# Local means of a pooling branch: shifted additions on GpSimd in place of products with banded matrices

## Chip, cores and metric

The kernel runs on one core of a Trainium2 chip. The metric is the device time of one execution in microseconds. Three runs of the kernel before took 1716.43, 1716.89 and 1719.67 us; their median is 1716.89 us.

## What is computed

The reference is a transformer of two layers over 256 latent tokens and 256 context tokens of width 1024, in float32. Each layer has a half feed-forward block, a mixing block and a second half feed-forward block. The mixing block projects the normalised tokens with `w_in` and puts three branches beside one another: neighbourhood attention (4 heads), a pooling branch (256 features), and grouped-query attention (GQA, 8 query heads, 2 key heads, with rotary positions on the latent tokens). `w_out` brings them back to 1024 features. In the last layer the context tokens only give keys and values, so pooling runs three times in all: for the latent and the context half in layer 0, and for the latent half in layer 1.

The pooling branch is what the change touches. Its 256 features fall into four groups of 64 with windows of 2, 4, 8 and 16 tokens:

```python
def _pool_mix(u, w_pool, scale):
    ...
    lo = jnp.clip(t - win // 2, 0, n)
    hi = jnp.clip(t - win // 2 + win, 0, n)
    sums = cs[:, hi, g_idx] - cs[:, lo, g_idx]
    mean = sums / (hi - lo).astype(jnp.float32)[None, :, :, None]
    y = (mean - u32.reshape(bn, n, POOL_GROUPS, POOL_GC)).astype(u.dtype)
    y = jnp.einsum('blgc,gcd->blgd', y, w_pool)
    return y.reshape(bn, n, POOL_WIDTH) * scale
```

Here `cs` is the running sum of u over the tokens. For each token the mean over a window of its neighbours is taken, u itself is subtracted, and each group is multiplied by a 64 x 64 matrix and scaled.

## The kernel before

The code names the engines PE (TensorE), ACT (ScalarE), DVE (VectorE), POOL (GpSimd) and SP (the queue that loads the weights). Activations lie with features on partitions and tokens along the row; columns 0 to 255 are the latent half (v = 0) and 256 to 511 the context half (v = 1). The large products are done three times over (`mm3`, L344 to L351): weights and activations are split into a high part and the rest, both in a reduced float32, and high x high, high x rest and rest x high are added up. Weights come from HBM into a raw buffer and are split into a slot by ACT (the high part, L306) and DVE (the rest, L309). `take` asks for the next slot in the order in which `attn_stream` (L607) queued them, and `done` gives a slot back and starts the next split.

The order of the work on each engine is the order in which the program issues it. A planner in the builder sets it: `tick` (L105) advances a clock by the estimated PE time of each product, and `later(us, fn)` issues a step when that clock has come to its due time.

In `attention` (L675), the keys, the queries of neighbourhood attention and its values `va` come first. Then `run` (L928) goes through a list of jobs. In layer 0 there are six of neighbourhood attention, then twelve of GQA; in layer 1 four and eight. For each job n the scores are issued (`scores`, L824, with the products in L838 and L839 and the softmax in `soft`), then filler work for as long as the table FILL says, and then `flip` (L867), which transposes the probabilities of job n - 2 on PE and copies them on ACT (L886). At the end of job n the queries of jobs n + 1 and n + 2 are split (`queries`, L815; L725 on ACT and L726 on DVE) if they are ready.

The filler work comes in pieces from `piece` (L1048). First comes `rest_in` (L964), the projections that are left:

- four q chunks of 128 features for GQA, each of 24 products of 512 columns (256 in layer 1) and yielded in four pieces. ACT takes each out of PSUM (L978) and squares it (L980); its statistics are taken on PE 3.0 later (L985).
- After every two chunks, `q_post(j)` is due 3.0 later. It calls `rotate` (L731): a product with a rotation matrix on PE (L736), a product with the sines on DVE (L739), a product with the cosines on POOL (L740), and, due 1.5 later, their addition on DVE (L743). Then `norm`, due 2.0 later, takes a reciprocal square root by a chain of small DVE instructions (L388 to L397, and L960). GQA jobs of a chunk wait for it by the flag `turned`.
- u, by `token_major` (L791): with tokens on partitions, one block of 128 tokens at a time, activations as the stationary operand and the weights as the moving one, 24 products of 256 columns for each block.

When `rest_in` has ended, pieces are `pv` (L901, the product of probabilities and values), `pooled` for each half, the products of modulation (L181, weights `w_ada` from HBM by SP, L157) and `rest_out` (L993), which multiplies what does not depend on GQA with `w_out`.

`pooled(v)` (L1007) multiplies u by banded matrices that hold the window weights minus the identity: for each group two products of 128 x 128 (L1015) and two of 8 columns (L1016, L1017) for the windows that reach over the boundary of the two token blocks. These are plain float32. The result is copied by ACT to y (L1020); 3.0 later `fin` multiplies it by the pooling weights (L1025), and ACT and DVE scale and split the result (L1029, L1030). The bands come by two loads for each layer (L808) into two temporary buffers, and the edges by one (L642).

POOL also clears the zero halves of the key tiles (`key_tile`, L707; the GQA keys at job 2) and other buffers, and issues some loads.

Of the kernel before, what the change touches and what calls it, by code (L numbers as in the profile page):

```python
# [9 lines left out]
F32 = mybir.dt.float32  # L10
# [26 lines left out]
T2K = 12  # L37
# [13 lines left out]
def dit_kernel(  # L51
# [2 lines left out]
    x, c, ctx_in, c_ctx, w_ada, b_ada, norm_g,  # L54
    ffn1_up, ffn1_down, ffn2_up, ffn2_down, w_in, w_out,
    na_rpb, pool_w, pool_scale, q_norm_g, k_norm_g, final_g,
    k_ident, k_rot, k_rope, k_mask, k_pool, k_edge,
    out,
):
    nc = tc.nc  # L60
# [25 lines left out]
    gsc = const.tile([128, 6, KD, 2], F32, name="gsc")  # L86
    hgt = const.tile([128, 4, KD, 2], F32, name="hgt")
    bm = const.tile([128, 2048], F32, name="bm")
    edge = const.tile([128, 2, 4, 8], F32, name="edge")
    pwbd = const.tile([128, 2, 128], F32, name="pwbd")  # L90

    def mm_bank(dt=F32):
        return ps_mm.tile([128, 512], dt, tag="mm", name="mm")
# [32 lines left out]
    def add_main(src3, shape, splits):  # L126
        stream.append(("main", src3, shape, splits))
# [228 lines left out]
    def acol(a, k, lo, hi):  # L356
        return a[:, 0, k, lo:hi], a[:, 1, k, lo:hi]
# [249 lines left out]
    def attn_stream(l, ada=()):  # L607
        ada = list(ada)
        w = w_in[l]
        c0 = lambda v: v[:, :, 0:128]  # L610
        c1 = lambda v: v[:, :, 128:256]
        k0 = lambda v: v[:, 0:4, :]
        k1 = lambda v: v[:, 4:8, :]

        def blk(lo):
            return w[:, lo:lo + 256].rearrange("(k p) f -> p k f", p=128)

        def fill():
            if ada:
                add_ada(*ada.pop(0))  # L620
        add_main(blk(256), (KD, 256), [c0, c1])
        add_main(blk(1536), (KD, 256), [c0, c1])
        add_main(blk(0), (KD, 256), [c0, c1])
        add_main(blk(512), (KD, 256), [k0, k1])
        for j in range(2):
            srcs = [w[:, 1024 + t * 256 + j * 128:1024 + t * 256 + j * 128 + 128].rearrange("(k p) f -> p k f", p=128) for t in range(2)]
            cc = [lambda v, i=i: v.rearrange("p k (t c) -> p (k t) c", t=2)[:, :, i * 64:(i + 1) * 64] for i in range(2)]
            add_main(srcs, (KD, 256), cc)
        add_main(blk(768), (KD, 256), [k0, k1])
        for part in range(2):  # L630
            for dq in range(2):
                for _ in range((0, 4, len(ada), 0)[2 * part + dq]):
                    fill()
                src = w_out[l][part * 512:(part + 1) * 512, dq * 512:(dq + 1) * 512].rearrange("(k p) d -> p k d", p=128)
                add_main(src, (4, 512), [lambda v: v[:, :, 0:256], lambda v: v[:, :, 256:512]])

    def attn_prep(l):

        if l == 0:
            ACT.dma_start(out=mask, in_=k_mask)  # L640
            ACT.dma_start(out=rot, in_=k_rot)
            ACT.dma_start(out=edge, in_=k_edge)  # L642
# [32 lines left out]
    def attention(l, a, both):  # L675
# [8 lines left out]
        def carve(n, pat, **kw):  # L684
            r = B[:, o0[0]:o0[0] + n].rearrange(pat, **kw)
            o0[0] += n
            return r
        va = carve(1024, "p (b f) -> p b f", b=4)
        u = carve(1024, "p (b f) -> p b f", b=4)
        qc = carve(2048, "p (c t) -> p c t", c=4)  # L690
        kc = carve(512, "p t -> p t")
        vc = carve(512, "p (b f) -> p b f", b=4)
        vcT = carve(512, "p t -> p t")
        A = a["t"]
        bmv = bm.rearrange("p (t h k) -> p t h k", t=2, h=4)
        O = [None]
# [105 lines left out]
        for _ in token_major(va, 4):  # L802
            pass


        pmd = [tmp.tile([128, 512], F32, tag="t2k", bufs=T2K, name="pmd") for _ in range(2)]
        for b in range(2):
            ACT.dma_start(out=pmd[b].rearrange("p (g t) -> p g t", g=4), in_=k_pool[b])  # L808


        rq8 = small.tile([128, 40], F32, tag="rq8", bufs=1, name="rq8")
# [151 lines left out]

        def rest_in():  # L964

            qst.append(mm_bank())
            for j in range(2):
                sl = [take(), take()]
# [17 lines left out]
                    later(3.0, qstat)  # L986
                    yield
                later(3.0, lambda j=j: q_post(j))
            yield from token_major(u, nb)

        gate = modT[:, l * 72 + 40:l * 72 + 48, :]

# [12 lines left out]
                done()  # L1005

        def pooled(v):  # L1007
            ps = mm_bank()
            pv_ = ps.rearrange("p (c t) -> p c t", c=2)
            for g in range(4):  # L1010
                r0 = 64 * (g % 2)
                o = pv_[r0:r0 + 64, g // 2, :]
                ug = [u[:, 2 * v + tb, g * 64:(g + 1) * 64] for tb in range(2)]
                for tb in range(2):
                    PE.matmul(out=o[:, tb * 128:(tb + 1) * 128], lhsT=ug[tb], rhs=pmd[tb][:, g * 128:(g + 1) * 128], start=(g < 2 and tb == 0), stop=False)  # L1015
# [6 lines left out]
            def fin():
                ps2 = mm_bank()
                for ch in range(2):
                    PE.matmul(out=ps2[:, ch * TX:(ch + 1) * TX], lhsT=pwbd[:, ch, :], rhs=y[:, ch * TX:(ch + 1) * TX], start=True, stop=True)  # L1025
                for ch in range(2):
                    s = colsB[:, 104 + 2 * l + ch:105 + 2 * l + ch]
                    oh, ol = acol(O[0], 2 + ch, v * TX, v * TX + TX)
                    ACT.activation(out=oh, in_=ps2[:, ch * TX:(ch + 1) * TX], func=AF.Copy, scale=s)  # L1029
                    DVE.scalar_tensor_tensor(out=ol, in0=ps2[:, ch * TX:(ch + 1) * TX], scalar=s, in1=oh.bitcast(F32), op0=ALU.mult, op1=ALU.subtract)  # L1030
                missing[0] -= 1
# [268 lines left out]
def _constants():  # L1300
# [17 lines left out]
    kcol = np.arange(64)  # L1318
    w0 = np.clip(col - 8, 0, 48)[:, None]
    mask = ((kcol[None] >= w0) & (kcol[None] < w0 + 16)).astype(np.uint32)  # L1320
    pool = np.zeros((256, 4, 256), np.float32)
    for g, w in enumerate((2, 4, 8, 16)):
        for t in range(256):
            lo, hi = max(t - w // 2, 0), min(t - w // 2 + w, 256)
            pool[lo:hi, g, t] = np.float32(1.0) / np.float32(hi - lo)
            pool[t, g, t] -= np.float32(1.0)
    blocks = np.stack([pool[0:128, :, 0:128], pool[128:256, :, 128:256]])
    edge = np.stack([pool[0:128, :, 128:136], pool[128:256, :, 120:128]], axis=1)
    return {"k_ident": ident, "k_rot": rot, "k_rope": rope, "k_mask": mask, "k_pool": np.ascontiguousarray(blocks), "k_edge": np.ascontiguousarray(edge)}
# [27 lines left out]
```

## Time and profile before

| what | value |
|---|---|
| median of three runs | 1716.89 us |
| the profiled execution's own time | 1716.95 us |
| its span in the trace | 1715.2 us |
| granted clock, mean | 0.99 |
| PE busy | 1675.8 us, 98% of the span |
| DVE busy | 1024.0 us, 60% |
| ACT busy | 663.5 us, 39% |
| POOL busy | 40.0 us, 2% |

The span is counted from the first instruction to the last; the 1.75 us between it and the execution's time lie around them. Times in rows of the profile are microseconds from the span's start unless marked ns. In a row of the timeline the first number is the start, the second the length, then come the engine, the line of the kernel, the operation, output and inputs with their size, the count, and in brackets the idle time before it with what ended it. Matmuls overlap in these rows: the time that one costs is the distance from its start to that of the next. Layer 0's mixing block runs from about 395 to 600 us, layer 1's from about 1341 to 1500 us. The program's names `q`, `u`, `va` and others are parts of one tile, and show up as `qkv`.

### The profile page before, as it was taken

To read this page: it belongs to the slowest core of one execution; us is meant where nothing else is said; L and a number is where in the kernel's file an instruction comes from. 1 tells how busy PE (TensorE), PEld (TensorE's weight loads), DVE (VectorE), ACT (ScalarE), POOL (GpSimd) and SP (SyncE) were. 2 spreads that over 40 slices of the span, in tenths; PEclk is the share of its full clock that TensorE was granted. 3 is DMA by queue.
4 is the path that set the end of the run, shared out by engine and by line. 5 is a ranking of instruction groups with operands and counts; after the bars stand their busy time and mean duration, and the time that the engine had idled before them with its cause. 6 is when DMAs were issued, how large, how long until landed. Compare 5 with 4: busy or idle time off the path is not lost.

```text
span 1715.2 us, 23680 instructions
## 1 busy us (share of the span) xinstructions
PE 1675.8 (98%) x9512; PEld 1420.5 (83%) x9512; DVE 1024.0 (60%) x1748; ACT 663.5 (39%) x1087; POOL 40.0 (2%) x60
## 2 busy tenths in 40 slices
PE   6999999999999999999999999999999999989998
PEld 4778888889886798888888898888888987779998
DVE  5667666666555676665764567545434656565554
ACT  4432223324556643223233243223222356644443
POOL 0000200000010000000000000020000000000000
PEclk8999999999999999999999999999999999989999
DMA  9755556531305325453653334555433134556561
GB/s 319 207 166 172 161 161 189 166 129 50 111 28 193 107 67 184 148 154 135 184 178 99 98 105 166 160 154 180 134 99 98 50 111 148 185 139 193 171 198 50
DMA packets 295335, 246.48 MB, mean 144 GB/s; under 512 B 9377, under 2 KB 262442, under 8 KB 293176
## 3 DMA queue, kind: packets, MB, share of 16 engines
q1 hardware_dynamic: 292680, 241.30, 45.6%
q0 software_dynamic: 1088, 2.15, 0.5%
q8 instruction: 75, 1.23, 0.3%
q10 hardware_dynamic: 1456, 1.52, 0.3%
q14 instruction: 36, 0.29, 0.1%
HBM read 243.88 MB, written 2.00 MB: 143 GB/s over the span
## 4 chain that ended last, share of the span: by engine, by line
PE 90%; DVE 4%; DMA 3%; ACT 2%; issue 1%; SPq 0%; DVEq 0%; ACTq 0%
PE mm L348 27%; PE mm L350 27%; PE mm L349 27%; PE mm L912 1%; PE aux L878 1%; DVE w L309 1%; DMA raw<-in_w_ada_dram 1%; DMA ada_raw<-in_w_ada_dram 1%; PE ada L181 1%; PE mm L838 1%; PE mm L839 1%; DVE ada_acc L221 1%; PE ada L229 1%; ACT w L306 1%; PE aux L409 0%
## 5 line engine op out<-in xcount | busy, mean ns | idle before, releaser
L348 PE MATMUL mm<-act,w 128*128 128x512 f32 (+1 forms) x2592 | 910.4, 351 | 5.7 <-ACT act L437 3.3
L350 PE MATMUL mm<-act,w 128*128 128x512 f32 (+1 forms) x2592 | 903.3, 348 | 1.9 <-DVE w L309 1.9
L349 PE MATMUL mm<-act,w 128*128 128x512 f32 (+1 forms) x2592 | 903.4, 349 | 1.1 <-DVE act L431 0.9
L348 PEld LDWEIGHTS mm<-act,w 128*128 128x128 f32 x2592 | 493.2, 190 | 86.7 <-issue 15.9
L350 PEld LDWEIGHTS mm<-act,w 128*128 128x128 f32 x2592 | 493.1, 190 | 64.4 <-DVE w L309 2.5
L349 PEld LDWEIGHTS mm<-act,w 128*128 128x128 f32 x2592 | 493.4, 190 | 63.1 <-DVE act L431 1.6
L309 DVE TENSOR_TENSOR w<-raw,w 128x1024 fp32r<-128x1024 f32 (+1 forms) x312 | 371.1, 1199 | 244.5 <-ACT w L306 243.9
L306 ACT CAST w<-raw 128x1024 fp32r<-128x1024 f32 (+1 forms) x312 | 315.0, 1023 | 120.5 <-PE mm L350 98.4
L221 DVE SCALAR_TENSOR_TENSOR ada_acc<-ada_raw,sc,ada_acc 128x512 f32<-128x512 f32 x308 | 216.1, 746 | 50.9 <-DMA ada_raw<-in_w_ada_dram 27.3
L558 ACT CAST act<-gf 128x512 fp32r<-128x512 f32 (+1 forms) x87 | 49.7, 572 | 317.5 <-DVE gf L555 317.5
L461 DVE SCALAR_TENSOR_TENSOR hT<-mm,hgt,hT 128x256 f32<-128x256 f32 x168 | 75.1, 480 | 96.9 <-PE mm L350 96.6
L552 ACT ACTIVATE sil<-mm 128x512 f32<-128x512 f32 (+1 forms) x87 | 47.7, 548 | 214.2 <-PE mm L350 204.1
L555 DVE TENSOR_TENSOR gf<-sil,mm 128x512 f32<-128x512 f32 (+1 forms) x87 | 54.4, 625 | 93.5 <-PE mm L350 77.7
L559 DVE TENSOR_TENSOR act<-gf,act 128x512 fp32r<-128x512 f32 (+1 forms) x87 | 54.9, 631 | 55.5 <-ACT act L558 55.5
L374 ACT ACTIVATE sq<-hT 128x256 f32<-128x256 f32 (+1 forms) x52 | 25.6, 492 | 108.5 <-DVE hT L461 108.5
L437 ACT ACTIVATE act<-nt,modT 128x256 fp32r<-128x256 f32 x88 | 43.4, 508 | 49.4 <-DVE nt L436 49.3
L219 ACT ACTIVATE ada_acc<-ada_raw,sc 128x512 f32<-128x512 f32 x44 | 29.6, 717 | 47.9 <-DMA ada_raw<-in_w_ada_dram 37.1
L855 DVE TENSOR_REDUCE nm<-mm 128x1 f32<-128x512 f32 (+1 forms) x60 | 41.0, 686 | 4.4 <-PE mm L839 3.7
L863 ACT ACTIVATE P<-mm,nm,rq 128x512 f32<-128x512 f32 (+1 forms) x48 | 33.7, 708 | 21.9 <-DVE nm L860 18.9
L431 DVE SCALAR_TENSOR_TENSOR act<-nt,modT,act 128x256 fp32r<-128x256 f32 x88 | 41.3, 480 | 1.3 <-ACT act L437 1.3
L436 DVE SCALAR_TENSOR_TENSOR nt<-hT,gsc,aux 128x256 f32<-128x256 f32 x88 | 40.8, 476 | 1.8 <-PE aux L416 1.2
L660 POOL DMA_DIRECT2D braw<-tab x32 | 19.5, 619 | 780.7 <-DVE gf L555 604.3
(149 smaller groups left out, 885.4 us busy)
## 6 DMA issues: line engine op xcount, KB each, us to landing
raw<-in_ffn_up_dram SPq DMA_DIRECT2D x172, 512.0 KB
ada_raw<-in_w_ada_dram SPq DMA_DIRECT2D x192, 256.0 KB
raw<-in_ffn_down_dram SPq DMA_DIRECT2D x32, 1024.0 KB
raw<-in_w_ada_dram SPq DMA_DIRECT2D x16, 1024.0 KB
raw<-in_ffn_down_dram SPq DMA_DIRECT2D x16, 768.0 KB
raw<-in_w_in_dram SPq DMA_DIRECT2D x10, 1024.0 KB
raw<-in_w_out_dram SPq DMA_DIRECT2D x8, 1024.0 KB
raw<-in_w_ada_dram SPq DMA_DIRECT2D x12, 512.0 KB
```

What stands on the lines that cost most here:

```text
L221: DVE.scalar_tensor_tensor(out=o, in0=raw, scalar=col, in1=o, op0=ALU.mult, op1=ALU.add)
L306: ACT.copy(out=wh, in_=sl)
L309: DVE.tensor_tensor(out=wl, in0=sl, in1=wh.bitcast(F32), op=ALU.subtract)
L348: PE.matmul(out=ps, lhsT=wh, rhs=ah, start=start and i == 0, stop=False)
L349: PE.matmul(out=ps, lhsT=wh, rhs=al, start=False, stop=False)
L350: PE.matmul(out=ps, lhsT=wl, rhs=ah, start=False, stop=stop and i == last)
L437: ACT.activation(out=acol(a, k, v * TX, v * TX + TX)[0], in_=t, func=AF.Identity, bias=modT[:, l * 72 + 3 * n * 8 + k, v:v + 1])
L461: DVE.scalar_tensor_tensor(out=hT[:, k, cols], in0=ps, scalar=gate[:, k, v:v + 1], in1=hT[:, k, cols], op0=ALU.mult, op1=ALU.add)
L552: ACT.activation(out=s[:, 0:n], in_=pa[:, 0:n], func=AF.Silu)
L555: DVE.tensor_tensor(out=u[:, 0:n], in0=s[:, 0:n], in1=pb[:, 0:n], op=ALU.mult)
L558: ACT.copy(out=gh, in_=uv)
L559: DVE.tensor_tensor(out=gl, in0=uv, in1=gh.bitcast(F32), op=ALU.subtract)
```

## The change

u is now projected with features on partitions, as the q chunks are, and ahead of them: two chunks of 128 features with 24 products of 512 columns each (256 in layer 1), in four pieces each. Its weights move ahead of those of q in the queue of weights. ACT copies the result into rows of 272 columns for each half, of which 8 on each side are zero.

The window sums are then shifted additions along these rows on POOL, in `window_means`, which is issued at the start of the first q piece, for each half. Sums of 2 come from u and u shifted by one; sums of 4 from two sums of 2; sums of 8 from two of 4; sums of 16 from two of 8. Each group's sum is multiplied by a table of reciprocal counts, and u is subtracted; the result takes u's place. `pooled` then has only the product with the pooling weights left, without the copy of y and without the wait of 3.0, and the planner charges 0.86 for it in place of 1.7 (its second product was not charged before). The loads of bands and edges go; a table of 256 KB is loaded for each layer. Two small memsets on POOL clear the margins of u.

```diff
@@ attn_stream
         add_main(blk(512), (KD, 256), [k0, k1])
+        add_main(blk(768), (KD, 256), [c0, c1])
         for j in range(2):
...
-        add_main(blk(768), (KD, 256), [k0, k1])
@@ attention
-        u = carve(1024, "p (b f) -> p b f", b=4)
+        u = carve(4 * UW, "p (c v t) -> p c v t", c=2, v=2)
+        sums1 = carve(2 * UW, "p (c t) -> p c t", c=2)
+        sums2 = carve(2 * UW, "p (c t) -> p c t", c=2)
...
-        pmd = [tmp.tile([128, 512], F32, tag="t2k", bufs=T2K, name="pmd") for _ in range(2)]
-        for b in range(2):
-            ACT.dma_start(out=pmd[b].rearrange("p (g t) -> p g t", g=4), in_=k_pool[b])
+        ACT.dma_start(out=count, in_=k_count)
+        for p0 in (0, UW - 8):
+            POOL.memset(u[:, :, :, p0:p0 + 8], 0.0)
+
+        def window_means(v):
+            uv, lo, hi = u[:, :, v], slice(0, 64), slice(64, 128)
+            inner = slice(8, 8 + TX)
+            def add(o, a, b):
+                POOL.tensor_tensor(out=o, in0=a, in1=b, op=ALU.add)
+            add(sums1[:, :, 1:272], uv[:, :, 0:271], uv[:, :, 1:272])
+            add(sums2[:, :, 2:271], sums1[:, :, 1:270], sums1[:, :, 3:272])
+            means = [(lo, 0, sums1), (hi, 0, sums2), (lo, 1, sums1), (hi, 1, sums2)]
+            for i, (r, ch, src) in enumerate(means):
+                if i == 2:
+                    add(sums1[:, 1, 4:269], sums2[:, 1, 2:267], sums2[:, 1, 6:271])
+                if i == 3:
+                    add(sums2[hi, 1, 8:264], sums1[hi, 1, 4:260], sums1[hi, 1, 12:268])
+                o = src[r, ch, inner]
+                POOL.tensor_tensor(out=o, in0=o, in1=count[r, ch], op=ALU.mult)
+                POOL.tensor_tensor(out=uv[r, ch, inner], in0=o, in1=uv[r, ch, inner], op=ALU.subtract)
@@ rest_in
+            for ch in range(2):
+                s = take()
+                ps = mm_bank()
+                for k in range(KD):
+                    mm3(ps[:, 0:nx], [(wcol(s, k, 0), acol(A, k, 0, nx))], nx, k == 0, k == KD - 1)
+                    if k % 2 == 1 and k < KD - 1:
+                        yield
+                done()
+                ACT.copy(out=u[:, ch, 0:nx // TX, 8:8 + TX], in_=ps[:, 0:nx].rearrange("p (v t) -> p v t", t=TX))
+                yield
+            for v in halves(both):
+                window_means(v)
             qst.append(mm_bank())
...
-            yield from token_major(u, nb)
@@ pooled
-            for g in range(4):
...
-                for tb in range(2):
-                    PE.matmul(out=o[:, tb * 128:(tb + 1) * 128], lhsT=ug[tb], rhs=pmd[tb][:, g * 128:(g + 1) * 128], start=(g < 2 and tb == 0), stop=False)
...
-            tick(1.7)
-            y = tmp.tile([128, 512], F32, tag="t2k", bufs=T2K, name="y")
-            ACT.copy(out=y, in_=ps)
...
+            ps2 = mm_bank()
+            for ch in range(2):
+                PE.matmul(out=ps2[:, ch * TX:(ch + 1) * TX], lhsT=pwbd[:, ch, :], rhs=u[:, ch, v, 8:8 + TX], start=True, stop=True)
+            tick(0.86)
...
-            later(3.0, fin)
```

More of the change, by code (lines that the diff above doesn't have):

```diff
@@ L18 @@
 KD = 8
+UW = 272
 TX = 256
@@ L56, in dit_kernel @@
     na_rpb, pool_w, pool_scale, q_norm_g, k_norm_g, final_g,
-    k_ident, k_rot, k_rope, k_mask, k_pool, k_edge,
+    k_ident, k_rot, k_rope, k_mask, k_count,
     out,
@@ L88, in dit_kernel @@
     bm = const.tile([128, 2048], F32, name="bm")
-    edge = const.tile([128, 2, 4, 8], F32, name="edge")
     pwbd = const.tile([128, 2, 128], F32, name="pwbd")
@@ L641, in attn_prep @@
             ACT.dma_start(out=rot, in_=k_rot)
-            ACT.dma_start(out=edge, in_=k_edge)
             ACT.dma_start(out=rope, in_=k_rope.rearrange("s p t -> p s t"))
@@ L693, in attention @@
         vcT = carve(512, "p t -> p t")
+        count = carve(512, "p (c t) -> p c t", c=2)
         A = a["t"]
@@ L1007, in pooled @@
         def pooled(v):
-            ps = mm_bank()
-            pv_ = ps.rearrange("p (c t) -> p c t", c=2)
-            for g in range(4):
-                r0 = 64 * (g % 2)
-                o = pv_[r0:r0 + 64, g // 2, :]
-                ug = [u[:, 2 * v + tb, g * 64:(g + 1) * 64] for tb in range(2)]
-                for tb in range(2):
-                    PE.matmul(out=o[:, tb * 128:(tb + 1) * 128], lhsT=ug[tb], rhs=pmd[tb][:, g * 128:(g + 1) * 128], start=(g < 2 and tb == 0), stop=False)
-                PE.matmul(out=o[:, 128:136], lhsT=ug[0], rhs=edge[:, 0, g, :], start=False, stop=False)
-                PE.matmul(out=o[:, 120:128], lhsT=ug[1], rhs=edge[:, 1, g, :], start=False, stop=(g >= 2))
-            tick(1.7)
-            y = tmp.tile([128, 512], F32, tag="t2k", bufs=T2K, name="y")
-            ACT.copy(out=y, in_=ps)
[L1022 to L1031, printed above, removed]
-            later(3.0, fin)
+            ps2 = mm_bank()
+            for ch in range(2):
+                PE.matmul(out=ps2[:, ch * TX:(ch + 1) * TX], lhsT=pwbd[:, ch, :], rhs=u[:, ch, v, 8:8 + TX], start=True, stop=True)
+            tick(0.86)
+            for ch in range(2):
+                s = colsB[:, 104 + 2 * l + ch:105 + 2 * l + ch]
+                oh, ol = acol(O[0], 2 + ch, v * TX, v * TX + TX)
+                ACT.activation(out=oh, in_=ps2[:, ch * TX:(ch + 1) * TX], func=AF.Copy, scale=s)
+                DVE.scalar_tensor_tensor(out=ol, in0=ps2[:, ch * TX:(ch + 1) * TX], scalar=s, in1=oh.bitcast(F32), op0=ALU.mult, op1=ALU.subtract)
+            missing[0] -= 1
         def steps(gen, us):
@@ L1320, in _constants @@
     mask = ((kcol[None] >= w0) & (kcol[None] < w0 + 16)).astype(np.uint32)
-    pool = np.zeros((256, 4, 256), np.float32)
+    count = np.zeros((128, 2, 256), np.float32)
     for g, w in enumerate((2, 4, 8, 16)):
[L1323 to L1329, printed above, removed]
+        t = np.arange(256)
+        n = np.minimum(t - w // 2 + w, 256) - np.maximum(t - w // 2, 0)
+        count[64 * (g % 2):64 * (g % 2) + 64, g // 2] = np.float32(1.0) / n.astype(np.float32)
+    return {"k_ident": ident, "k_rot": rot, "k_rope": rope, "k_mask": mask, "k_count": count}
 _INS = ['x', 'c', 'ctx', 'c_ctx', 'w_ada', 'b_ada', 'norm_g', 'ffn1_up', 'ffn1_down', 'ffn2_up', 'ffn2_down',
         'w_in', 'w_out', 'na_rpb', 'pool_w', 'pool_scale', 'q_norm_g', 'k_norm_g', 'final_g']
-_CONST = ['k_ident', 'k_rot', 'k_rope', 'k_mask', 'k_pool', 'k_edge']
+_CONST = ['k_ident', 'k_rot', 'k_rope', 'k_mask', 'k_count']
 _OUTS = [((1, 256, 1024), 'float32')]
```

## Prediction

> **What bounds the kernel now.** I read the page first, then the busy time by stretches, then the timeline around every piece of work that the diff touches, and last the POOL groups.
>
> ```profile
> span 1715.2 us, 23680 instructions
> PE 1675.8 (98%) x9512; PEld 1420.5 (83%) x9512; DVE 1024.0 (60%) x1748; ACT 663.5 (39%) x1087; POOL 40.0 (2%) x60
> ...
> PE 90%; DVE 4%; DMA 3%; ACT 2%; issue 1%; SPq 0%; DVEq 0%; ACTq 0%
> ```
>
> TensorE is the bound: 98% of the span busy and 90% of the chain that ended last. POOL does almost nothing. A mean says little of one stage, so I looked at the stretches in which the first layer's attention runs (columns: length, then busy time of PE, PEld, DVE, ACT, POOL).
>
> ```profile
> 480.00:500.00 20.00, 20.00 (x140) 18.47 (x140) 12.60 (x40) 13.61 (x35) 3.05 (x2) 1.00 0.16 53
> 500.00:520.00 20.00, 20.00 (x179) 16.54 (x178) 11.93 (x31) 11.89 (x27) 0.00 (x0) 1.00 0.15 53
> ```
>
> There PE has no idle time at all, at a granted clock of 1.00. So products taken from PE here shorten the program one for one, and a wait put in front of PE lengthens it one for one. The change does both.
>
> **The change: what PE loses.** The banded products of the two halves of layer 0, from their first matmul to the next work on PE, and those of layer 1:
>
> ```profile
> 514.47 0.65 PE L1015 MATMUL mm<-pmd,qkv 128*64 128x128 f32 x4
> ...
> 516.72 1.09 PE L883 MATMUL aux<-ident,P 128*128 128x128 f32 x8
> ...
> 518.67 0.65 PE L1015 MATMUL mm<-pmd,qkv 128*64 128x128 f32 x4
> ...
> 520.91 1.13 PE L1025 MATMUL mm<-y,pwbd 128*128 128x256 f32 x4
> 521.98 1.08 PE L912 MATMUL mm<-PT,qkv 128*64 128x256 f32 x8
> ...
> 1430.49 0.96 PE L1015 MATMUL mm<-pmd,qkv 128*64 128x128 f32 x4
> ...
> 1433.06 1.09 PE L878 MATMUL aux<-ident,P 128*128 128x128 f32 x8
> ```
>
> 516.72 - 514.47 = 2.25, 520.91 - 518.67 = 2.24 and 1433.06 - 1430.49 = 2.57 us: 7.06 us go. The product with the pooling weights (521.98 - 520.91 = 1.07 us each) stays. The copy of y on ACT and the two loads of the bands per layer go too; ACT was busy 11.89 of 20 us there, so that is worth nothing by itself. Two temporary buffers and a PSUM bank are held less long, which could only take a wait away, and PE has none there: nothing. If ACT's or DVE's cover fails, the price is in the waits below.
>
> The projection of u changes shape. With tokens on partitions it is 96 matmuls of 256 columns in layer 0, exactly the shape of va; with features on partitions it is 48 of 512, the shape of the q chunks. The first matmul of va and what follows its last, and 18 matmuls of a q chunk with what follows:
>
> ```profile
> 446.43 0.28 PE L348 MATMUL mm<-w,act 128*128 128x256 f32 x1
> ...
> 457.94 0.40 PE L838 MATMUL mm<-K,qst 128*128 128x512 f32 x1
> ...
> 458.87 0.39 PE L348 MATMUL mm<-act,w 128*128 128x512 f32 x1
> ...
> 462.95 0.39 PE L838 MATMUL mm<-K,qst 128*128 128x512 f32 x1
> ```
>
> 96 take 457.94 - 446.43 = 11.51 us. 18 of 512 take 4.08, so 48 take 10.88: 0.63 us less. In layer 1 both forms are 48 of 256 columns: nothing. PE loses 7.06 + 0.63 = 7.7 us.
>
> **The change: what is moved.** u now comes ahead of the q chunks. Each chunk is four pieces of the fill for the planner, and u is eight pieces (8 x 1.28 us of the planner's clock) in place of eight of nearly the same size, so the slots stay: in layer 0 pieces 1 to 3 lie after the scores of job 0, 4 and 5 after job 1, 6 to 13 after job 2, 14 after job 3, 15 to 17 after job 4, 18 and 19 after job 5. Before, q chunk 1 ended with piece 8 and its rotation was long done when job 6, the first GQA job, wants it. Now q chunk 1 ends with piece 16, where chunk 3 did, and q_post(0), due 3.0 later on the planner's clock, is issued where q_post(1) was, behind the scores of job 5. That place, with the scores of job 6 at 498.54:
>
> ```profile
> 492.94 0.83 ACT L725 CAST qst<-qkv 64x256 fp32r<-64x256 f32 x2
> ...
> 493.12 0.95 PE L985 MATMUL mm<-hind,qsq 128*128 128x2 f32 x8
> 493.38 0.87 DVE L726 TENSOR_TENSOR qst<-qkv,qst 64x256 fp32r<-64x256 f32 x2 [1.39 <-ACT qst L725]
> 493.93 1.11 PE L736 MATMUL aux<-qkv,rot 128*128 128x256 f32 x4
> ...
> 495.07 0.69 DVE L739 TENSOR_TENSOR rot_t<-aux,rope 128x512 f32<-128x512 f32 x1 [0.82 <-PE aux L736]
> 495.18 1.30 POOL L740 TENSOR_TENSOR qkv<-qkv,rope 128x512 f32<-128x512 f32 x1 [15.79 <-PE aux L736]
> 495.68 1.28 DVE L855 TENSOR_REDUCE nm<-mm 128x2 f32<-128x512 f32 x2
> ...
> 497.21 0.68 DVE L743 TENSOR_TENSOR qkv<-qkv,rot_t 128x512 f32<-128x512 f32 x1
> ...
> 497.81 0.17 DVE L388 TENSOR_SCALAR rs_v<-mm 128x16 f32<-128x16 f32 x1
> ...
> 498.38 1.07 ACT L886 COPY PT<-aux 128x512 f32<-128x512 f32 x2
> ...
> 498.54 0.47 PE L838 MATMUL mm<-K,qst 128*128 128x512 f32 x1
> ...
> 500.19 0.17 DVE L960 TENSOR_SCALAR rq<-rs_y 128x16 f32<-128x16 f32 x1
> ...
> 500.48 0.29 DVE L891 COPY rec<-sums 128x256 f32<-128x256 f32 x1
> ```
>
> Here job 6's scores had their queries (L725, L726) already. After the change those queries are split only behind the rotation, the reciprocal root (L388 to the end of L960, 2.55 us), the reciprocal of the sums and its copy (0.5, by the copy's 0.29 and a start of as much as L960's) and the ACT copies of the flip. All of it stands in DVE's one queue.
>
> PE's slot for job 6 first moves forward: by then one of two rotations (1.11 us) and two of four query statistics (493.93 - 493.12 = 0.81 us each) have not yet come, so it is 498.54 - 2.7 = 495.8, and the rotation's matmuls end at 493.93 + 1.11 - 2.7 = 492.3. With a free POOL: L739 to 493.2, the two maxima (1.28) to 494.5, L743 to 495.2, the root to 497.75, reciprocal and copy to 498.25, L726 to 499.1. PE would wait 499.1 - 495.8 = 3.3 us. That is the lower bound.
>
> **The change: what POOL gains.** One half takes 12 tensor_tensor instructions: 542 + 538 + 265 + 256 elements of additions, and four products and four subtractions of 256, 3649 elements per partition. POOL's only rows of this kind:
>
> ```profile
> L740 POOL TENSOR_TENSOR qkv<-qkv,rope 128x512 f32<-128x512 f32 x4 | 5.2, 1298 | 43.8 <-PE aux L736 43.8
> ...
> L740 POOL TENSOR_TENSOR qkv<-qkv,rope 128x256 f32<-128x256 f32 x2 | 3.4, 1687 | 64.3 <-ACT w L306 64.3
> ...
> 436.69 4.04 DVE L309 TENSOR_TENSOR w<-raw,w 128x1024 fp32r<-128x1024 f32 x3 [1.12 <-ACT w L306]
> 436.83 1.69 POOL L740 TENSOR_TENSOR qkv<-qkv,rope 128x256 f32<-128x256 f32 x1 [32.05 <-ACT w L306]
> ...
> 474.30 0.68 ACT L978 ACTIVATE qkv<-mm,colsB 128x512 f32<-128x512 f32 x1
> ```
>
> 1298 ns for 512 elements is 2.54 ns each: 9.25 us a half, 18.5 for layer 0. The other form took 1687 ns for half the elements, beside L309 on DVE: 1.04 us more than half of 1298. By the lesser row the two halves take 18.5 us, by the greater 48 us (6.6 ns each). I take the lesser, since few DVE instructions with two SBUF inputs lie in this place (one L309 behind piece 16), plus 1.0 for that one and 0.8 for the pads' memsets and the 24 starts: 20.3.
>
> The Trainium skill, in "GPSIMD Engine Reference", section 3.1, has 4497 ns for 2048 fp32 elements of such an addition, so an estimate of 8.0 us a half in place of 9.25: by that page the sum would be 1.5 us less, 1714.1 us (POOL free 2.5 us sooner, the wait down to its lower bound of 3.3); its section 4.1 tells one not to do elementwise work there at all, as about twice as slow as VectorE. "SBUF — State Buffer", section "Who interferes with whom", says that a DVE instruction with two SBUF inputs and a reading GpSimd instruction lock each other out; the row at 436.83 agrees.
>
> POOL starts when u's second chunk is out of PSUM. That copy stands in ACT's queue where L978 does at 474.30; with one activation less ahead of it, it ends at about 474.4. So POOL is busy to 474.4 + 20.3 = 494.7. The rotation's product (L740) is queued behind it, ends at 496.0, and DVE's in-order queue (add, root, reciprocal, L726) waits for it: 496.0 + 0.7 + 2.55 + 0.5 + 0.9 = 500.6. PE waits 500.6 - 495.8 = 4.8 us.
>
> **Layer 1** has the same shift: 6 pieces lie after job 0, 5 after job 1, 7 after job 2, 6 after job 3, so q chunk 1 (piece 16) ends after job 2, q_post(0) falls into job 3's scores, and the first GQA job is job 4.
>
> ```profile
> 1425.15 1.11 PE L736 MATMUL aux<-qkv,rot 128*128 128x256 f32 x4
> ...
> 1433.75 1.07 ACT L886 COPY PT<-aux 128x512 f32<-128x512 f32 x2
> 1433.90 0.48 PE L838 MATMUL mm<-K,qst 128*128 128x512 f32 x1
> ```
>
> The next two are of the chain in order of time, and of the waits of PE in layer 1's attention:
>
> ```profile
> 1436.13 8.04 DMA raw<-in_w_ada_dram
> ```
>
> ```profile
> PE ada L181 <- DMA raw<-in_w_ada_dram: 1.2, 1, 1.2
> ```
>
> More work lies between here (six pieces, pooled, one modulation product), and POOL has one half only. It also has the memset of the GQA keys behind that half, as they come later in program order, but both end before DVE gets to the add. What is left is ACT: the flip's copies end 1434.82 - 1433.90 = 0.9 us after PE's slot, and the split of the queries takes another 1.3 (494.25 - 492.94): PE waits 2.2 us. On the other hand the planner charges pooled 0.86 in place of 1.7, so a modulation product is run a job earlier and its refill, which stands on the chain for 8 us, starts sooner; that wait is worth between 0 and 1.2 us, I take 0.6.
>
> **Sum:** -7.7 + 4.8 + 2.2 - 0.6 = -1.3 us. The profiled execution took 1716.95 us, the median of the runs 1716.89, so I make no correction: 1715.6 us. A measurement of this kernel can tell about 0.2% (3.4 us) from no change; this is inside.
>
> **Rivals.** A, the gain stays: the queries are ready in time, because the pieces fall otherwise than I walked them (one more piece or a pv ahead of job 6, three ahead of job 4). For it: PE has no idle time here now, so ACT and DVE keep up with these pieces. Against it: 499.1 - 492.3 = 6.8 us from the rotation's matmuls to the end of L726 even with a free POOL, against 495.8 - 492.3 = 3.5 us of PE work. Time: 1716.95 - 7.7 - 0.6 = 1708.7, and with half the waits 1712.
>
> B, POOL becomes the bound of layer 0's middle: if its instructions meet DVE at the port, or dependent ones start late, the rotation waits for them, and every microsecond past 494.7 is one of PE. At 1.4 times the row (26 us and the same 1.8) POOL is free at 502.1, 7.4 us later: 1715.6 + 7.4 = 1723.0. It is decided at 4.7 us, 12.5 us a half, from where the result is over 0.2% slower. For it: the row of 1687 ns. Against it: the row of 1.30 at 495.18 ran beside DVE's L739 and L855, which read PSUM, and was no longer than the mean of its kind.
>
> **How the numbers follow.** The forecast has 0.48, A 0.29, B 0.23. The forecast's own bounds: in layer 0 waits from 3.3 (POOL free) to 8.5 (POOL a fifth slower than the row, 3.7 us later); in layer 1 from 1.3 (the split alone) to 3.3 (one more block of 1.04 as at 436.83); the refill 0 to 1.2. So from 1716.95 - 7.7 + 4.6 - 1.2 = 1712.7 to 1716.95 - 7.7 + 11.8 = 1721.0, mostly within 0.2%. Faster by over 0.2%: A and a little of the forecast, 0.31. Slower: B, 0.23. Same: 0.46. The range leaves out the better half of A and the worse of B: 1710.5 to 1722.
>
> **What would show it.** In the changed profile: the L1015 to L1017 rows gone; POOL rows of about 1.4 us (271 x 2 elements) and 0.65 (256); POOL's last one near 494; ahead of job 6's scores (L838) a PE idle time of 3 to 6 us released by the query split, and one of about 2 ahead of job 4's in layer 1. No idle there means A; 8 us or more, with POOL the releaser of DVE's add, means B. It is wrong altogether if PE's products of u are not at 0.227 us a matmul.

## The result, and the profile after

The kernel after takes 1735.78 us (median of 4 runs, 1734.90 to 1736.56) against 1716.93 before: a ratio of 1.0111, 95% interval 1.0099 to 1.0123, that is 18.9 us slower. The forecast was 1715.6, with 1722.0 as the upper end. The profiled execution of after took 1736.56 us. From its page:

```profile
span 1734.8 us, 23422 instructions
...
PE 1678.7 (97%) x9368; PEld 1418.1 (82%) x9368; DVE 1025.4 (59%) x1745; ACT 662.2 (38%) x1085; POOL 70.3 (4%) x100
...
PE 86%; DVE 6%; ACT 3%; DMA 2%; issue 2%; POOL 1%; SPq 0%; ACTq 0%; DVEq 0%; POOLq 0%
```

PE has 144 instructions fewer, and is yet busy for longer. POOL gained 30 us, but has only 1% of the chain. The stretches of after in both layers' attention:

```profile
480.00:500.00 20.00, 18.53 (x114) 16.12 (x112) 8.03 (x13) 12.76 (x33) 18.24 (x23) 1.00 0.16 53
500.00:520.00 20.00, 16.09 (x80) 12.32 (x82) 10.97 (x32) 10.50 (x21) 0.00 (x0) 0.83 0.15 52
520.00:540.00 20.00, 15.52 (x96) 9.29 (x93) 12.09 (x37) 9.06 (x22) 3.35 (x3) 0.91 0.17 54
1430.00:1450.00 20.00, 15.28 (x99) 12.84 (x99) 11.43 (x27) 11.08 (x25) 7.93 (x10) 0.85 0.38 133
1450.00:1470.00 20.00, 17.71 (x104) 10.53 (x103) 9.75 (x32) 9.13 (x22) 1.28 (x1) 0.80 0.50 184
```

The same stretches of before that the prediction does not show (layer 1's lie some 11 us earlier there):

```profile
520.00:540.00 20.00, 20.00 (x127) 12.89 (x126) 9.87 (x22) 12.64 (x30) 0.32 (x1) 1.00 0.61 212
1420.00:1440.00 20.00, 19.90 (x165) 16.25 (x167) 14.96 (x45) 12.02 (x26) 1.30 (x1) 1.00 0.37 123
1440.00:1460.00 20.00, 18.66 (x134) 13.75 (x127) 11.70 (x31) 15.15 (x36) 0.00 (x0) 1.00 0.49 194
```

Before, PE was busy for all of layer 0's stretches and idle for 1.4 us in layer 1's, at a clock of 1.00 throughout. After, PE idles 1.47 + 3.91 + 4.48 = 9.9 us in layer 0 and 4.72 + 2.29 = 7.0 us in layer 1; and the granted clock falls, which makes busy time longer without showing as a wait. Busy time multiplied by the missing share of the clock gives an estimate of it: 16.09 x 0.17 + 15.52 x 0.09 = 4.1 us and 15.28 x 0.15 + 17.71 x 0.20 = 5.8 us.

The losses can be placed by two landmarks on POOL that both kernels have, first of before, then of after:

```profile
403.68 1.09 POOL L707 MEMSET K<- 64x512 f32 x2 [7.09 <-PE mm L350]
...
1133.07 9.77 POOL L660 DMA_DIRECT2D braw<-tab  x16 [604.26 <-DVE gf L555]
```

```profile
404.92 1.09 POOL L709 MEMSET K<- 64x512 f32 x2 [7.10 <-PE mm L350]
...
1144.40 9.81 POOL L659 DMA_DIRECT2D braw<-tab  x16 [615.86 <-DVE gf L555]
```

Between them, where layer 0's mixing lies, 729.39 us became 739.48 (+10.1); from there to the span's end, with layer 1, 582.1 became 590.4 (+8.3); 1.2 arose ahead of both, where nothing was changed. Idle time plus slow clock less the products that went (4.5 + 0.6 us in layer 0, 2.6 in layer 1) gives 9.9 + 4.1 - 5.1 = +8.9 and, with the 1.4 us of idle time that layer 1 had there before, 7.0 - 1.4 + 5.8 - 2.6 = +8.8: close to the +10.1 and +8.3. Another 1.5 us in layer 0 (5.26 x 0.28) is slow clock behind a wait of 1.34 us that both kernels have, in the stage of the keys, which the change does not touch. In before, then in after:

```profile
436.00:442.00 6.00, 6.00 (x28) 4.97 (x29) 5.28 (x5) 3.83 (x5) 1.69 (x1) 1.00 0.48 137
436.00:442.00 6.00, 5.26 (x18) 4.31 (x19) 4.87 (x6) 4.72 (x7) 1.27 (x3) 0.72 0.25 71
```

So the question is what PE waited for, and why the clock fell. PE's timeline in after:

```profile
503.91 0.79 PE L859 MATMUL mm<-K,qst 128*128 128x512 f32 x1 [5.38 <-DVE qst L728]
504.50 0.63 PE L860 MATMUL mm<-K,qst 128*128 128x512 f32 x1
...
508.77 0.48 PE L349 MATMUL mm<-act,w 128*128 128x512 f32 x1
...
531.36 0.41 PE L940 MATMUL aux<-ident,rec 128*128 128x128 f32 x2 [1.19 <-DVE rec L912]
...
535.50 0.66 PE L899 MATMUL aux<-ident,P 128*128 128x128 f32 x4 [3.29 <-ACT rec L941]
...
1442.55 0.58 PE L1018 MATMUL mm<-hind,qsq 128*128 128x2 f32 x4 [1.58 <-ACT qkv L1011]
...
1448.41 0.80 PE L859 MATMUL mm<-K,qst 128*128 128x512 f32 x1 [2.47 <-DVE qst L728]
...
1464.89 1.97 PE L899 MATMUL aux<-ident,P 128*128 128x128 f32 x8 [2.29 <-ACT PT L907]
```

The first wait in each layer (5.38 and 2.47) is the one that was forecast, for the queries of the first GQA job (L859 is L838 of before). Behind the first, matmuls of 512 columns start 0.43 us apart (504.50 and its followers), not 0.227, up to 508.77: about 11 of them cost 0.2 us more each. The Trainium skill, "TensorE: Matmul & The Clock Gate", Part 1, says that the array falls to half its clock when it has been idle for about 3.4 us and comes back after as long at work; the spacing agrees, and here it was 4.9 us of work until the full clock was back.

The waits of 1.19 and 3.29 were not forecast. Their chain on DVE and on ACT, in after:

```profile
528.34 0.17 DVE L388 TENSOR_SCALAR rs_v<-mm 128x16 f32<-128x16 f32 x1
...
530.64 0.17 DVE L981 TENSOR_SCALAR rq<-rs_y 128x16 f32<-128x16 f32 x1
...
530.92 0.29 DVE L912 COPY rec<-sums 128x256 f32<-128x256 f32 x1
531.13 0.68 DVE L876 TENSOR_REDUCE nm<-mm 128x1 f32<-128x512 f32 x1
```

```profile
532.13 0.78 ACT L884 ACTIVATE P<-mm,nm,rq 128x512 f32<-128x512 f32 x1 [3.26 <-DVE nm L881]
...
534.71 0.47 ACT L1047 ACTIVATE act<-mm,colsB 128x256 fp32r<-128x256 f32 x1 [0.55 <-DVE act L1048]
535.08 0.36 ACT L941 COPY rec<-aux 128x256 f32<-128x256 f32 x1
```

`q_post(1)`, for the third and fourth chunk, is later too (its product on POOL starts at 523.18 in place of 495.18, that of `q_post(0)` at 498.62 in place of 478.09), so its root (L388 to L981, 2.5 us) and the copy of the sums' reciprocals (L912), for which PE waits the 1.19 us, now stand in DVE's queue ahead of a job's maxima. ACT waits 3.26 us for those, does the exponentials, then the pooled outputs (which no longer come 3.0 later), and only then the copy that frees the bank PE wants at 535.50. POOL's part, with its last instructions and DVE behind them:

```profile
477.15 2.25 POOL L818 TENSOR_TENSOR qkv<-qkv 128x542 f32<-128x542 f32 x2 [7.84 <-ACT qkv L995]
...
491.38 1.63 POOL L828 TENSOR_TENSOR qkv<-qkv 64x256 f32<-64x256 f32 x1
...
497.81 0.73 POOL L829 TENSOR_TENSOR qkv<-qkv 64x256 f32<-64x256 f32 x1
498.62 1.27 POOL L742 TENSOR_TENSOR qkv<-qkv,rope 128x512 f32<-128x512 f32 x1
```

```profile
499.92 0.69 DVE L745 TENSOR_TENSOR qkv<-qkv,rot_t 128x512 f32<-128x512 f32 x1 [3.10 <-POOL qkv L742]
```

### The profile page after: what moved, and what is told of

Same layout as the page of the kernel before. It is cut to its first block, busy times and chain, and to the rows that moved or that the text cites. A ratio compares the mean times of both kernels' runs of the same rounds, so it can differ in the third digit from the quotient of the medians.

```text
span 1734.8 us, 23422 instructions
## 1 busy us (share of the span) xinstructions
PE 1678.7 (97%) x9368; PEld 1418.1 (82%) x9368; DVE 1025.4 (59%) x1745; ACT 662.2 (38%) x1085; POOL 70.3 (4%) x100
## 4 chain that ended last, share of the span: by engine, by line
PE 86%; DVE 6%; ACT 3%; DMA 2%; issue 2%; POOL 1%; SPq 0%; ACTq 0%; DVEq 0%; POOLq 0%
PE mm L348 26%; PE mm L349 26%; PE mm L350 26%; PE mm L933 1%; DVE w L309 1%; PE aux L899 1%; PE ada L181 1%; DVE ada_acc L221 1%; ACT w L306 1%; PE ada L229 1%; PE mm L859 1%; ACT K L716 1%; PE mm L860 1%; DMA raw<-in_w_ada_dram 1%; DMA ada_raw<-in_w_ada_dram 0%
## 5 line engine op out<-in xcount | busy, mean ns | idle before, releaser
L348 PE MATMUL mm<-act,w 128*128 128x512 f32 (+1 forms) x2624 | 922.2, 351 | 5.8 <-ACT act L437 3.3
L350 PE MATMUL mm<-act,w 128*128 128x512 f32 (+1 forms) x2624 | 914.7, 349 | 1.9 <-DVE w L309 1.9
L349 PE MATMUL mm<-act,w 128*128 128x512 f32 (+1 forms) x2624 | 915.3, 349 | 1.0 <-DVE act L431 0.9
L348 PEld LDWEIGHTS mm<-act,w 128*128 128x128 f32 x2624 | 499.8, 190 | 88.1 <-issue 15.1
L350 PEld LDWEIGHTS mm<-act,w 128*128 128x128 f32 x2624 | 499.5, 190 | 65.3 <-DVE w L309 2.6
L349 PEld LDWEIGHTS mm<-act,w 128*128 128x128 f32 x2624 | 499.9, 190 | 64.1 <-DVE act L431 1.6
L309 DVE TENSOR_TENSOR w<-raw,w 128x1024 fp32r<-128x1024 f32 (+1 forms) x312 | 372.1, 1202 | 249.5 <-ACT w L306 248.9
```

The source lines that it names most:

```text
L309: DVE.tensor_tensor(out=wl, in0=sl, in1=wh.bitcast(F32), op=ALU.subtract)
L348: PE.matmul(out=ps, lhsT=wh, rhs=ah, start=start and i == 0, stop=False)
L349: PE.matmul(out=ps, lhsT=wh, rhs=al, start=False, stop=False)
L350: PE.matmul(out=ps, lhsT=wl, rhs=ah, start=False, stop=stop and i == last)
```

## The experiments

Three theories. O: the new order is what costs; with u ahead of the q chunks both `q_post` come later, and PE waits for queries and, through DVE's and ACT's queues, for banks. P: POOL's 21 us cost by themselves, by what is queued behind them and by slower instructions on DVE. C: the slow clock behind each wait is a cost of its own. All ratios are to the kernel before, measured beside it on the same chip; 0.001 is 1.7 us.

| kernel | median us | ratio, 95% |
|---|---|---|
| after | 1735.78 | 1.0111 (1.0099 to 1.0123) |
| e1_no_bands | 1711.66 | 0.9972 (0.9960 to 0.9984) |
| e2_no_means | 1729.74 | 1.0082 (1.0065 to 1.0099) |
| e3_u_between | 1723.74 | 1.0049 (1.0034 to 1.0064) |
| e4_busy_pe | 1731.06 | 1.0089 (1.0074 to 1.0104) |
| f1_u_last | 1715.66 | 0.9996 (0.9986 to 1.0007) |
| f2_u_last_means | 1742.35 | 1.0154 (1.0137 to 1.0171) |
| f3_between_root_later | 1722.04 | 1.0037 (1.0026 to 1.0049) |
| f4_root_later | 1732.30 | 1.0098 (1.0083 to 1.0113) |
| g1_u_last_held | 1739.15 | 1.0135 (1.0118 to 1.0152) |
| g2_u_last_outputs_late | 1712.05 | 0.9981 (0.9971 to 0.9990) |
| g5_between_late_held | 1722.35 | 1.0032 (1.0019 to 1.0045) |
| h1_outputs_late | 1736.13 | 1.0117 (1.0100 to 1.0134) |

**e1_no_bands**: the kernel before, with the banded products left out.

```diff
-                    PE.matmul(out=o[:, tb * 128:(tb + 1) * 128], lhsT=ug[tb], rhs=pmd[tb][:, g * 128:(g + 1) * 128], start=(g < 2 and tb == 0), stop=False)
...
-            ACT.copy(out=y, in_=ps)
+            ACT.copy(out=y.rearrange("p (b f) -> p b f", b=2), in_=u[:, 2 * v:2 * v + 2, :])
```

> The kernel before, with the banded products (L1015 to L1017) left out: y is copied from u as it stands, so that no local means are computed; all else, the order of the work and its due times, stays. If PE has no slack in this stage, the 7.1 us of the prediction's first term go: 1709.9 us. If the products only filled time in which PE would wait anyway, the time stays at 1717.

-4.8 us (-6.9 to -2.7). What the change removes is worth some 5 of the 7.1 us that its rows show; no gain of that size could pay for what follows.

**e2_no_means**: the kernel after without the additions on POOL, u as it is.

```diff
-            for v in halves(both):
-                window_means(v)
```

> The changed kernel, with window_means left out (the pooling weights multiply u itself), so POOL has nothing to do there; the order with u ahead of q stays. Theory O (the order: queries and roots come too late): the add of job 6's rotation no longer waits for POOL (3.0 us of the 5.4), the other waits stay: 1730 to 1733 us. Theory P (POOL's long work is the cause): nearly all of the loss goes, 1709 to 1713.

+14.1 us. Without POOL's work 5.0 of the 18.9 us go (1.0111 - 1.0082; with the two intervals, plus or minus 3.6). O holds for most of it (1729.74 is 0.3 under its range). The wait ahead of job 6 fell from 5.4 to 2.2 us; that of layer 1 did not fall (3.3 against 2.5).

**f1_u_last**: as e2_no_means, but u's two chunks behind the four q chunks, as the kernel before had them, in the weights' queue too.

```diff
-            for ch in range(2):
...
             qst.append(mm_bank())
             for j in range(2):
...
                 later(3.0, lambda j=j: q_post(j))
+            for ch in range(2):
...
```

> The kernel after with u's projection back behind the four query chunks, features on partitions, and without window_means (the pooling then multiplies u itself; nothing else is left out). Theory O (the order of the projections is what costs): the waits of the first grouped-query jobs are gone and the time is that of the kernel before without its banded products, 0.997 of the kernel before in the same call, 1709 to 1713 us. Rival S (u's new shape, its evictions on ScalarE or the pooling's outputs without their delay of 3 cost by themselves): 1716 us or more.

-0.7 us. e2_no_means and f1_u_last do the same work and differ in the place of u alone: 1.0082 - 0.9996 = 0.0086, 14.8 us (plus or minus 3.4). This is the price of the order. But theory O's figure was missed by 4 us against e1_no_bands, near S. The next run shows where these are.

**g2_u_last_outputs_late**: f1_u_last with the pooled product and its outputs due as before.

```diff
-            tick(0.86)
+            tick(1.7)
+            def fin():
...
+            later(3.0, fin)
```

> f1_u_last (u last, features on partitions, window_means left out) with the pooled product and its outputs due 3 us later and 1.7 us of the schedule's clock for the half, as in the kernel before. Theory Q (the 4 us between f1_u_last and e1_no_bands are the pooled outputs in ScalarE's queue ahead of the transposes' copies, 1.6 + 2.3 us of waits at TensorE): 0.9972 of the kernel before, 1709 to 1713 us, and the wait of 2.3 us in layer 1 gone. Rival: u's evictions in the new shape cost them: 1714 to 1717 us.

-3.3 us, and -2.6 against f1_u_last: the time that Q gives. u's shape costs little; the dropped delay of 3.0 costs some 2.6 us (plus or minus 2.4) in this order. The waits are less clear. Those of PE in f1_u_last, then in g2_u_last_outputs_late:

```profile
PE aux L899 <- ACT PT L907: 2.3, 1, 2.3
...
PE aux L899 <- ACT rec L941: 1.6, 1, 1.6
...
PE mm L1040 <- ACT qkv L1018: 1.2, 2, 0.7
```

```profile
PE aux L899 <- ACT PT L907: 1.7, 1, 1.7
...
PE aux L899 <- ACT rec L941: 1.5, 2, 0.9
```

What went for certain is the pooled product's own wait for u's copy (1.2); the wait of 2.3 was to go and fell to 1.7 only.

**e3_u_between**: u and its means, and u's weights in their queue, between the two pairs of q chunks.

```diff
                 later(3.0, lambda j=j: q_post(j))
+                if j == 0:
+                    for ch in range(2):
...
+                    for v in halves(both):
+                        window_means(v)
```

> The changed kernel, with u's two chunks and the window means between q chunks 1 and 2, so that q_post(0) has its old place and only q_post(1) is late; POOL does the same work. Theory O: the waits of 5.4 and 2.5 us ahead of the first GQA jobs go with the slow clock behind them, and those behind the second root (3.3 and 1.2 in layer 0, some 4 in layer 1) stay: 1718 to 1723 us. Theory P: POOL's work is as long, and now stands ahead of the second rotation: 1730 or more.

+8.4 us. With `q_post(0)` early again the waits of 5.4 and 2.5 us are gone, as O has it, and 10.6 us with them; the time is 0.7 us above O's range. In layer 1 the 2.3 us wait on the transposes' copy stays, and PE now waits 1.7 and 1.0 us for POOL. What is left in layer 0, in its PE timeline:

```profile
521.35 0.41 PE L941 MATMUL aux<-ident,rec 128*128 128x128 f32 x2 [1.19 <-DVE rec L913]
...
525.48 1.11 PE L900 MATMUL aux<-ident,P 128*128 128x128 f32 x4 [3.29 <-ACT rec L942]
```

These are the same waits, to 0.01 us, as at 531.36 and 535.50 in after. They hang on the second `q_post`, which is late in both. The next two test it.

**f4_root_later** and **f3_between_root_later**: after, and e3_u_between, each with one edit.

```diff
-            later(2.0, norm)
+            later((2.0, 5.0)[j], norm)
```

> The kernel after with that one edit (the second pair's root due 5 instead of 2 us behind its rotation); TensorE's, ScalarE's and GpSimd's instructions and their order stay as they are, only VectorE's 10 small instructions stand behind one job's softmax instead of ahead of it. Theory N: the wait of 3.3 us ahead of the transposes in layer 0 falls under 1.5 us, and the time is 1730 to 1733 us. Rival: 1735 to 1737 us, as the kernel after.

> The kernel with u between the two pairs of query chunks (e3_u_between), and the second pair's root and its copy to rq8 due 5 us behind its rotation instead of 2, which puts them behind one job's maxima on VectorE. Theory N (the late root chain ahead of job 8's maxima makes ScalarE's copy of the row sums late, and TensorE waits 3.3 + 1.2 us for the bank, with some 1.5 us of slow clock behind): 1718 to 1721 us. Rival: the copy is late for ScalarE's own queue, with the exponentials and the pooled outputs in it, and the time stays at 1723 to 1724 us.

-2.2 us against after and -2.1 against e3_u_between, each plus or minus 3.3, so neither is clear of noise by itself. f4_root_later's median is inside theory N's range; f3_between_root_later's 1722.04 lies between N's 1721 and the rival's 1723. In f4_root_later:

```profile
529.01 1.12 PE L899 MATMUL aux<-ident,P 128*128 128x128 f32 x4 [2.14 <-ACT rec L941]
```

The 1.19 is gone, but 3.29 only fell to 2.14, not under 1.5. So in the traces the late root accounts for about half of these waits (4.48 us became 2.14). The rest is put down to the same copy on ACT, which fits the rival's queue of exponentials and pooled outputs but does not by itself show it.

**e4_busy_pe**: the kernel after with 22 and 10 products into a spare bank ahead of the first GQA scores of the two layers. They add nothing to the result.

```diff
+                    if jobs[n][1] == "gqa" and ("na", 0) in K:
+                        spare = mm_bank()
+                        kt = K["na", 0]
+                        for _ in range((22, 10)[l]):
+                            PE.matmul(out=spare, lhsT=kt[:, 0, 0:128], rhs=kt[:, 1, :], start=True, stop=True)
                     late.append((jobs[n], scores(*jobs[n])))
```

> The changed kernel, with 22 (layer 0) and 10 (layer 1) matmuls of 512 columns into an unread bank ahead of the first GQA job's scores, 5.0 and 2.3 us at full clock, that is in the time in which PE waits for the queries. Theory C (a wait is followed by a slow clock, and that is a good part of the loss): the 5.4 us after job 6's scores run at 0.23 us a matmul in place of 0.43, and so in layer 1: 1730 to 1732.5 us. If the clock has another reason: 1735.8 or a little more.

-3.8 us against after (plus or minus 3.3), though PE has 32 products more. Its timeline (the first of the 22 lies just ahead of it):

```profile
496.67 4.96 PE L959 MATMUL mm<-K 128*128 128x512 f32 x21
501.97 0.50 PE L859 MATMUL mm<-K,qst 128*128 128x512 f32 x1 [0.34 <-DVE qst L728]
502.31 0.40 PE L860 MATMUL mm<-K,qst 128*128 128x512 f32 x1
502.54 0.40 PE L859 MATMUL mm<-K,qst 128*128 128x512 f32 x1
```

The scores still have to wait for their queries, but PE is at work meanwhile, and what follows runs 0.23 us apart at once. C holds: the slow clock is gone where PE was kept busy, and with it some 4 us. For layer 1 this is less certain: there the clock of after fell ahead of the wait that the products fill (last section), and in e4_busy_pe it did not, though the wait before it was as long (1.57 us).

**f2_u_last_means** and **g1_u_last_held**: u last with its means on POOL, and the pooled products held back. The diff is g1_u_last_held's. f2_u_last_means had 12 and 23 us, and a condition ending in `or not ada_todo`, a list that is empty in this stage, so that its hold did not take effect.

```diff
+                due.append(clock[0] + (14.0, 25.0)[v])
...
-            elif pools:
+            elif pools and clock[0] >= due[pools[0]]:
...
+        while pools:
+            pooled(pools.pop(0))
```

> As the run before, with window_means on GpSimd behind u's last eviction, and the two pooled products held back to 12 and 23 us of the schedule's clock behind it, with modulation products ahead of them instead. Theory O with GpSimd hidden: 1709 to 1714 us, since nothing waits for GpSimd. Rival P (21 us of GpSimd cost by themselves, through VectorE's slower instructions beside them or through the rotations queued behind, about 6 us as between the kernel after and the kernel after without means): 1715 to 1719 us.

> u last with window_means on GpSimd, and now the two pooled products really held back until 14 and 25 us of the schedule's clock behind the means' issue (in f2_u_last_means the hold did not take effect). Nothing is left out. Theory H (GpSimd's 21 us can hide behind the jobs when nothing waits for them): 1711 to 1716 us. Rival F (with the queries behind it and the output projection needing the pooled product, TensorE has only the jobs' own matmuls while GpSimd works, so that the jobs run at the pace of their softmax with slow clock): 1722 us or more, without a single wait for GpSimd.

+26.4 and +23.2 us: every theory was far off for the first. There PE stood in front of POOL:

```profile
PE mm L1043 <- POOL qkv L829: 23.0, 6, 7.7
```

In g1_u_last_held not one of PE's waits is put down to POOL, and it is hardly better. Its stretches while POOL works, and behind that:

```profile
520.00:530.00 10.00, 7.47 (x42) 4.69 (x40) 7.48 (x11) 6.14 (x13) 9.23 (x11) 0.95 0.66 265
530.00:540.00 10.00, 6.11 (x28) 4.41 (x28) 5.76 (x17) 8.03 (x21) 3.25 (x3) 0.71 0.01 2
...
550.00:560.00 10.00, 5.15 (x13) 3.80 (x13) 4.21 (x10) 4.09 (x13) 0.00 (x0) 0.66 0.00 0
```

This is what F forecast. Its reason is read from the kernel and was not tested alone: `rest_out` needs the pooled features, so with the means late there is little left to fill PE with between the jobs. Where u stood before, POOL's 21 us have no cover. Where u stands in after, they are covered but for the 5.0 us of e2_no_means, but the queries are late.

**g5_between_late_held**: f3_between_root_later with the delayed outputs of g2_u_last_outputs_late and the hold of g1_u_last_held.

> f3_between_root_later with the pooled product and its outputs due 3 us later as in the kernel before, and held until 14 and 25 us of the schedule's clock behind the means' issue (which takes effect in layer 1). Nothing is left out. Theory: the waits that are left at TensorE in f3_between_root_later (2.1 us for the copy of the sums in layer 0, 2.3 for the transposes' copy and 1.7 + 1.0 for GpSimd in layer 1) go, and with them the slow clock behind: 1713 to 1718 us. Rival: the rest of the loss lies elsewhere (VectorE beside GpSimd): 1720 to 1723 us.

+5.5 us, no different from f3_between_root_later: the rival's figure. The waits on POOL went and others came in layer 1, of 2.60 and 2.41 us; the first in PE's timeline:

```profile
1430.37 0.72 PE L1007 MATMUL mm<-hind,qsq 128*128 128x2 f32 x4 [2.60 <-ACT qsq L1002]
```

**h1_outputs_late**: the kernel after with the same delay of the outputs alone.

> The kernel after with one edit: the pooled product and its outputs due 3 us later, with 1.7 us of the schedule's clock for the half, as the kernel before had them. On ScalarE each pair of pooled outputs then stands one job later, in layer 1 behind one job's copy of the transposes, query split and exponentials. Theory Q (the dropped delay puts the pooled outputs into ScalarE's queue ahead of what TensorE waits for; 3.5 us between f1_u_last and g2_u_last_outputs_late): 1731 to 1733.5 us, with the waits of 3.3 us (layer 0) and 2.3 us (layer 1) ahead of the transposes under half of that. Rival (in the kernel after these waits hang on the late root and the late queries alone): 1735 us or more.

+20.1 us: no gain, so Q falls for this order. The 3.29 us wait fell to 2.12 and 1.58 grew to 2.44, with a new one of 1.24 in layer 1. The step pushed back on ACT only met other waits.

No version computes the whole result faster than the kernel before; the best, f3_between_root_later and g5_between_late_held, are 3 to 8 us slower. All versions keep the table FILL of the kernel before; whether another table, made for the new order, would win back part of the loss was not tried.

## Why the prediction was wrong, point by point

- *PE loses 7.7 us*: the rows are gone as said; left out alone, the bands brought 4.8 (2.7 to 6.9). Right in kind, a little large.
- *POOL is busy to 494.7*: to 498.54. The two halves took 498.54 - 477.15 = 21.4 against 20.3, but POOL began 2.75 us later than the forecast's 474.4: 1.2 us had arisen ahead of the block, and u's second copy (L995) waited on ACT behind the keys' split and two exponentials. PE's slot was late by as much (503.91 - 5.38 = 498.5 against 495.8), so the wait hardly changed.
- *PE waits 4.8 us ahead of job 6, 2.2 ahead of job 4*: 5.38 and 2.47. Mechanism, place and size right, though the lower bound was not: without POOL's work the first was 2.2 (e2_no_means), not 3.3. Rival A is out; B is not the cause either: POOL was 1.1 us over its price, not 7.4, and without it 14.1 of the 18.9 us stay.
- *Refill -0.6*: not a gain, by the trace. The modulation product that waited 1.18 us for its load no longer stands at its place, between one job's scores and the next transposes, and this wait is gone. But with nothing in that place PE waits 2.29 us for the copy ahead of these transposes (at 1464.89 above), with a slow clock behind. With the planner's old charge of 1.7 the wait is there too (2.30 in h1_outputs_late), so why it came stays open. The product in before:

```profile
1444.22 1.06 PE L181 MATMUL ada<-raw,sc 128*32 128x512 f32 x8 [1.18 <-DMA raw<-in_w_ada_dram]
```

- **The step that failed is the sum.** It let "a wait put in front of PE" lengthen the program "one for one" and ended with two waits of 7.0 us. Two terms were missing. First, the clock fell behind the waits: about 10 us of slow clock (4.1 + 5.8, estimated above), of which e4_busy_pe won back 3.8 at two waits. Second, "so the slots stay" was followed for `q_post(0)` alone. `q_post(1)`, moved by as much, was followed to no queue; nor were the pooled outputs, whose delay of 3.0 went. The waits that the sum lacks are those of 1.19, 3.29, 1.58 and 2.29 us, 8.4 us in all. The first three are of this kind. The 2.29 is that of the refill above, and the order alone does not make it: f1_u_last, with u last, has it too (2.27). Three runs that moved single steps (f3_between_root_later, f4_root_later, h1_outputs_late) each removed part of the 1.19 and 3.29, taken together, and none all; which share belongs to which step in the kernel after stays open. The 1.58 is in no version with u last, so it comes with the order, but by which step was not tested.
- Parts of the loss, as differences of the ratios (0.0111 is 19.1 us): 4.8 gained by the bands; 4.1 lost from e1_no_bands to f1_u_last (the pooled outputs' delay 2.6, the rest u's shape or chance); 14.8 by the order; 5.0 by POOL's work.

## What to carry to other kernels

When a step is moved ahead of others, follow every step that it pushes back, the second of a kind as well as the first, to its place in each engine's queue, and ask who stands behind it there. Price a wait of the bounding engine at its length plus what the clock loses behind it: here 17 us of waits cost an estimated 10 us more. Work taken off the bounding engine onto an idle one needs cover for its whole latency, between its input and the first reader, and the only cover here was the work whose results were needed next.

## What the runs showed of the hardware

The clock fell behind shorter waits than the 3.4 us that the Trainium skill gives in the place cited above, and here the measurement decides. In layer 1 of after it fell (the third number from the end) soon after the wait of 1.58 us, ahead of that of 2.47:

```profile
1441.00:1443.00 2.00, 0.45 (x4) 0.48 (x4) 1.90 (x6) 2.00 (x5) 0.00 (x0) 1.00 0.00 0
1443.00:1445.00 2.00, 2.00 (x15) 1.15 (x15) 1.73 (x10) 0.06 (x1) 0.00 (x0) 0.80 0.00 0
1445.00:1447.00 2.00, 0.94 (x5) 0.54 (x3) 1.46 (x3) 0.82 (x2) 0.00 (x0) 0.50 0.87 262
```

Read in stretches of 1 us, the half clock came in blocks of 3.42, 6.82, 10.24 and 3.42 us behind the moved steps of after; in the other traces there are also blocks of 13.64 and 20.48 (f2_u_last_means). All are close to whole multiples of 3.41. Waits of one length do not always get one: the 1.34 us wait in the stage of the keys has one of 3.42 in after and none in before, and the 2.3 us wait of layer 1 has one in after and none in f3_between_root_later. By these figures a block of 3.41 us in which PE is busy throughout costs half of its length, an estimated 1.7 us.

POOL's additions nearly kept their price (21.4 us against 20.3), but DVE beside them did not. POOL and DVE in e3_u_between:

```profile
1422.76 2.27 POOL L819 TENSOR_TENSOR qkv<-qkv 128x542 f32<-128x542 f32 x2 [2.50 <-ACT qkv L1020]
...
1422.85 1.03 DVE L396 TENSOR_TENSOR rs_t<-rs_t,rs_v 128x8 f32<-128x8 f32 x1
```

An instruction on 8 elements took 1.03 us in place of 0.17 (the same line at 1422.25), about until the first of POOL's two additions was done (2.27 us for both); and POOL's L828 at 491.38 took 1.63 us in place of 0.73 beside a DVE instruction of the weight split (L309 at 490.69, 1.72 us). This is the lock-out that the prediction cites from the Trainium skill ("SBUF — State Buffer", "Who interferes with whom"), which by this row holds for instructions of 8 elements too. Neither engine shows it as a wait.
